# A decoder step's feed-forward: sums moved between engines, a product block that starts on a copied bank, and a new ordering rule

## The chip, the cores and the metric

The kernel runs on one core of one Trainium2 chip. The metric is the device time of one execution in microseconds (us), as the median of several runs. The engines go by the names of the profile: PE multiplies matrices, ACT, DVE and POOL are the scalar, vector and general-purpose engines, SP starts most transfers. PSUM is the memory that PE writes its products to, in eight banks; SBUF is the working memory.

## What is computed

One step of a decoder layer for 512 prompt tokens and 32 sample tokens together (544 columns; the width is 1024). First come a mixing layer (attention and a recurrence) and a cross attention, which this change does not edit. Then follows the feed-forward, cut here from the reference:

```
u    = rmsnorm(x, norm_ffn)
ug   = u @ w_gate                              # 1024 x 2816
up   = concatenate([conv_buf, ug])
conv = conv_b + sum(conv_w[j] * up[:, j:j + T] for j in range(3))
x    = x + (silu(conv) * (u @ w_up)) @ w_down  # w_up 1024 x 2816, w_down 2816 x 1024
y    = rmsnorm(x, norm_final)
```

## The kernel before

Activations lie transposed, features on partitions and tokens along the free axis. Every fp32 product is made as three products in the faster fp32r format: each operand is split into a high part (a cast, on ACT) and a low part (operand minus high part, on DVE), and PE adds up high x high, high x low and low x high.

The 2816 hidden features are 22 tiles of 128. The first four gate tiles and the first four up tiles (`PLAIN`) are made directly: two halves of 256 and 288 columns each, 24 matmuls a half, with the row factor `r_ffn` (tile `r_ux` in the profile) put in when the bank is read. The other 18 gate and 18 up tiles are made in pairs (class `Pair`), by a seven-product scheme for 2x2 blocks: instead of eight block products, q1 to q7, 12 matmuls each, of which some use sums of blocks. On the activation side the blocks are called B11, B12, B21, B22, and the sums X, T, U, V (`blocks`, L1899); each is 128x544 in each of two parts `kp`. They are made once. Six tensors in each part need a high and a low part, and so does T. In the kernel before, the sums T and V and the low parts of T, V and B22 run on POOL (`ON_GPSIMD`, L1898), the rest on DVE. On the weight side S1 and S3 are added up by a transfer that accumulates, which POOL starts, and S2 and S4 by DVE.

Of a pair's outputs c11 = q1 + q2: ACT copies q1 out of bank `a` into SBUF (`kept`), q2 goes to a bank of its own (`d`), and DVE adds the two into the output tile. The block c12 is copied by ACT out of bank `a` (`c12_out`). c22 and c21 are made by DVE out of bank `c` and a kept copy. Bank `a` runs on: q1, q6, q5 and q3 all add up in it, with copies taken between. These banks come from a kind of five (`aux`); the down products use three others.

A gate tile then passes `conv` (L1760): a first tap on ACT, two taps on DVE, silu on ACT (tile `cv` in the profile). For the last tile the silu is recorded as one step with a load of the activation table set `LN_SET`, which the closing norm uses (L1778). An up tile passes `gated` (L1786): the product with the gate on POOL, 512 columns and 32 columns apart, then the split into h high and low. Last come the products with `w_down`, in groups of hidden tiles (`DOWNS`), as halves of 256 and 288 columns that DVE adds to x (tile `xr`), and for tiles 18 to 21 a closing stage (`last_half`, banks `ps_dz`) with the closing norm (`final`): a sum of squares over partitions on PE, Ln and Exp on ACT (`r_fin`, `r_final`), the products with y on DVE and POOL, and the transfers out.

**What sets the order.** The kernel is not emitted as written. Class `Tape` records every call as a step, with its tiles, an estimate of its length and its dependences. PE's main products keep the order in which they were recorded; for the feed-forward that order, `seq`, is written out by hand at the end (L2070 on). Everything else is ordered by a simulation in the recorder (`order`, L439): each engine starts the step that is due first (`begin`), due times run backwards from the products (`due`), and a step may start once it is due within its `lead` (15 us, or a value given for loads and splits). The simulation runs three times, each with the product times of the one before, and the last order is emitted. It also holds a picture of the SBUF port that DVE and POOL share: a DVE step of two kinds (`tensor_scalar`, `scalar_tensor_tensor`, with no PSUM operand) waits until POOL is free.

All of this happens before the launch; on the chip each engine runs its list in order and waits on semaphores. A tile that the change touches can therefore move others.

Of the kernel before, what the change touches and what calls it, by code (L numbers as in the profile page):

```python
# [17 lines left out]
SEQ = 512  # L18
# [231 lines left out]
class Tape:  # L250
# [7 lines left out]
    ROUNDS = 3  # L258
    BURST, PATIENCE, SLACK, LEAD = 1.0, 4.0, 12.0, 15.0
# [123 lines left out]
    def due(self):  # L383
# [18 lines left out]
        for s in reversed(self.steps):  # L402
            for u in s.users:
                if s in u.deps and not s.main:
                    s.begin = min(s.begin, u.begin - s.takes())

    def run(self):
# [3 lines left out]
        for s in self.mains:  # L411
            s.est = t
            t += s.length * scale
        for _ in range(self.ROUNDS):
            done = self.order()
            for s in self.mains:
                s.est = s.start
        for s in done:
            for call in s.calls:
                call()  # L420
# [3 lines left out]
    def order(self):  # L424
# [21 lines left out]
        now, clock, bus, todo, done, burst, first = 0.0, [0.0, 0.0], 0.0, len(self.steps), [], False, None  # L446

# [28 lines left out]
        def start(s):  # L476
# [13 lines left out]
            else:  # L490
                held_up = max(0.0, free["POOL"] - now) if s.port else 0.0
# [27 lines left out]
        while todo:  # L519
# [4 lines left out]
            for e in ("SP", "ACT", "DVE", "POOL"):  # L524
                if free[e] <= now + 1e-9:
                    at = clock[0] + min(now - clock[1], 4.0)
                    can = [s for s in waiting[e] if s.ready <= now + 1e-9 and s.begin <= at + (s.lead or self.LEAD) and fits(s)]
                    if can:
                        busy = free["POOL"] > now + 0.1
# [38 lines left out]
class _Engine:  # L568
# [5 lines left out]
    def __getattr__(self, method):  # L574
# [3 lines left out]
        def take(*args, **kw):  # L578
# [38 lines left out]
def tile_decoder_step(ctx: ExitStack, tc: tile.TileContext, xT, memT, kwT, vw, s0, conv_in, mkT, mv, vecs, cst,  # L617
# [1089 lines left out]
    dense_by_half(co_hl, KT, "co", co_evac, co_after)  # L1707
# [52 lines left out]
    def conv(j, deps):  # L1760
# [24 lines left out]
    def gated(j, deps):  # L1785

        def product():
            up, c = ups[j], hid[j]
            nc.gpsimd.tensor_tensor(up[:, :SEQ], up[:, :SEQ], c[:, :SEQ], op=ALU.mult)

        def product_s():
            up, c = ups[j], hid[j]
            nc.gpsimd.tensor_tensor(by_batch(up[:, SEQ:N]), by_batch(up[:, SEQ:N]), seg(c)[:, :, 0:4], op=ALU.mult)
# [8 lines left out]
        hi = job(high, job(product, *deps), job(product_s, *deps))  # L1802
# [3 lines left out]
    def load_a(name, src, k, lead=4.0):  # L1806
# [8 lines left out]
    def load_sum(name, a, b):  # L1815

        load, box = load_a(name, a, 4, lead=3.0)
# [3 lines left out]
        return job(lambda: None, job(accumulate, load, lead=4.0)), box  # L1821

    def split_a(name, box, k, ready, lead=6.0):
# [27 lines left out]
    def plain_tile(kind, j, i):  # L1851
# [3 lines left out]
        else:  # L1855
            load = job(lambda: ws.load(i, True), lead=9.0)
            split = job(lambda: ws.split_lo(i), job(lambda: ws.split_hi(i), load, lead=5.0),
                        lead=5.0)
        start = job(new_tile(kind, j), lead=6.0)
# [38 lines left out]
    ON_GPSIMD = ('T', 'V', 'B22')  # L1898

    def blocks(kp):  # L1900
# [27 lines left out]
        def low(name):  # L1928
            (nc.gpsimd if name in ON_GPSIMD else nc.vector).tensor_tensor(split(name, "l"), tok[name, kp]["t"], tok[name, kp]["h"].bitcast(F32),
# [14 lines left out]
    class Pair:  # L1944


        def __init__(self, kind, j, gates):
# [22 lines left out]
            first = job(load, lead=5.0)  # L1970
# [6 lines left out]
            for out, a, b in (("S2", "S1", "A11"), ("S4", "S2", "A12")):  # L1977
                self.w[out] = {}
                made[out] = job(lambda o=(out, a, b): self.add(*o), made[a], made[b], lead=8.0)
            self.low["A11"] = self.low["A12"] = job(low, job(high, first, lead=8.0), lead=8.0)  # L1980
# [243 lines left out]
```

## Time and profile before

| what | us |
|---|---|
| median of 3 runs | 848.43 (847.07 to 849.92) |
| the profiled execution | 845.8 |
| its span | 843.6 |
| PE busy in the span | 819.0 |
| DVE, ACT, POOL busy | 593.9, 403.6, 207.2 |
| activation table loads, 16 | 20.5 in all |

The profiled execution has 2.2 us around its span. A page of the profile gives the busy time of each engine, then the chain of work that ended last; further views group instructions by shape, list who waited for whom, or list the instructions in order of time. In a row of such a list the first number is the start, the second the duration, and what stands in brackets is how long the engine stood idle before it and whose end released it. Almost all instructions have the line of one helper (L612), so rows are told apart by the names of their tiles. As a guide to time: the mixing layer and the cross attention run to about 450 us, the plain tiles and the block sums to about 515, the pairs with the down products to about 806, and the closing stage to the end.

### The profile page before, as it was taken

To read this page: it belongs to the slowest core of one execution; us is meant where nothing else is said; L and a number is where in the kernel's file an instruction comes from. 1 tells how busy PE (TensorE), PEld (TensorE's weight loads), DVE (VectorE), ACT (ScalarE), POOL (GpSimd) and SP (SyncE) were. 2 spreads that over 40 slices of the span, in tenths; PEclk is the share of its full clock that TensorE was granted. 3 is DMA by queue.
4 is the path that set the end of the run, shared out by engine and by line. 5 is a ranking of instruction groups with operands and counts; after the bars stand their busy time and mean duration, and the time that the engine had idled before them with its cause. 6 is when DMAs were issued, how large, how long until landed. Compare 5 with 4: busy or idle time off the path is not lost.

```text
span 843.6 us, 18802 instructions
## 1 busy us (share of the span) xinstructions
PE 819.0 (97%) x7594; PEld 766.1 (91%) x7594; DVE 593.9 (70%) x1201; ACT 403.6 (48%) x798; POOL 207.2 (25%) x293
## 2 busy tenths in 40 slices
PE   9999999999999989999999988999999999999894
PEld 9989977888789879999889988999999999999894
DVE  6783735875988896564667987877867867768843
ACT  7412333543456454444545545454544634646625
POOL 1220000210210220222224863213222332333213
PEclk9999999999999999999999999999999999999998
DMA  9656797957932625260721345445565565465203
GB/s 333 210 137 191 251 293 244 302 158 226 302 87 77 206 79 187 61 220 23 247 85 50 95 132 137 131 123 150 149 150 139 138 162 148 128 175 162 74 1 107
DMA packets 90759, 132.32 MB, mean 157 GB/s; under 512 B 6064, under 2 KB 60080, under 8 KB 90544
## 3 DMA queue, kind: packets, MB, share of 16 engines
q1 hardware_dynamic: 84480, 120.69, 44.6%
q0 software_dynamic: 5184, 9.44, 6.9%
q8 instruction: 59, 0.97, 0.4%
q10 hardware_dynamic: 1008, 0.99, 0.3%
q14 instruction: 28, 0.23, 0.1%
HBM read 123.03 MB, written 8.07 MB: 155 GB/s over the span
## 4 chain that ended last, share of the span: by engine, by line
PE 81%; DVE 11%; ACT 3%; issue 2%; DMA 2%; POOL 1%; SPq 0%; DVEq 0%; POOLq 0%; ACTq 0%
PE ps_d L612 12%; PE ps_ag L612 6%; PE ps_wo L612 6%; PE ps_au L612 6%; PE ps_hv L612 3%; PE ps_k L612 3%; PE ps_co L612 3%; PE ps_cq L612 3%; PE ps_cu L612 3%; PE ps_cg L612 3%; PE ps_v L612 3%; PE ps_hq L612 2%; PE ps_hg L612 2%; PE ps_dz L612 2%; PE ps_hf L612 2%
## 5 line engine op out<-in xcount | busy, mean ns | idle before, releaser
L612 ACT CAST wh<-wr 128x1024 fp32r<-128x1024 f32 (+1 forms) x68 | 60.9, 908 | 102.0 <-PE ps_k L612 16.9
L612 POOL TENSOR_TENSOR up<-up,cv 128x512 f32<-128x512 f32 (+1 forms) x44 | 45.8, 1051 | 138.9 <-ACT cv L612 109.6
L612 DVE TENSOR_TENSOR wl<-wr,wh 128x1024 fp32r<-128x1024 f32 (+1 forms) x68 | 71.9, 1068 | 10.4 <-ACT wh L612 10.3
L612 POOL TENSOR_TENSOR hG<-hG,hf 128x256 f32<-128x256 f32 (+1 forms) x28 | 26.1, 933 | 189.8 <-DVE hf L612 134.9
L612 DVE TENSOR_TENSOR xr<-xr,ps_d 128x256 f32<-128x256 f32 x80 | 34.4, 433 | 25.4 <-PE ps_d L612 24.7
L612 DVE SCALAR_TENSOR_TENSOR cv<-ug,vec,cv 128x560 f32<-128x560 f32 x44 | 37.5, 853 | 1.5 <-ACT cv L612 1.1
L612 POOL COPY last<-ug 128x16 f32<-128x16 f32 (+1 forms) x44 | 15.6, 402 | 72.2 <-ACT ug L612 57.5
L612 ACT ACTIVATE cv<-cv 128x560 f32<-128x560 f32 x22 | 14.8, 674 | 30.5 <-DVE cv L612 30.5
L612 POOL TENSOR_TENSOR acc_cx<-acc_cx,sq_cx 128x256 f32<-128x256 f32 (+1 forms) x14 | 11.7, 839 | 56.5 <-ACT sq_cx L612 56.4
L612 ACT ACT_TABLE_LOAD x16 | 20.5, 1283 | 2.4 <-issue 2.2
L612 ACT ACTIVATE cv<-ug,vec 128x560 f32<-128x560 f32 x22 | 18.9, 860 | 3.9 <-POOL ug L612 2.8
L612 ACT ACTIVATE P<-P,mx 128x128 f32<-128x128 f32 (+3 forms) x32 | 17.6, 551 | 4.5 <-DVE mx L612 4.4
L612 PE MATMUL ps_co<-coh,wh 128*128 128x256 f32 (+1 forms) x64 | 18.9, 295 | 0.0
L612 PE MATMUL ps_co<-coh,wl 128*128 128x256 f32 (+1 forms) x64 | 18.4, 288 | 0.0
L612 PE MATMUL ps_co<-col,wh 128*128 128x256 f32 (+1 forms) x64 | 18.4, 288 | 0.0
L612 DVE TENSOR_TENSOR xr<-xr,ps_wo 128x256 f32<-128x256 f32 (+1 forms) x16 | 6.8, 435 | 15.1 <-PE ps_wo L612 15.1
L612 POOL COPY ug<-conv_state 128x16 f32<-128x16 f32 x22 | 17.1, 782 | 0.0
L612 ACT COPY keptu<-ps_au 128x272 f32<-128x272 f32 x18 | 7.0, 389 | 20.3 <-PE ps_au L612 19.6
L612 POOL TENSOR_TENSOR acc_ux<-acc_ux,sq_ux 128x256 f32<-128x256 f32 (+1 forms) x14 | 11.5, 820 | 20.4 <-ACT sq_ux L612 20.4
L612 PE MATMUL psd<-st,qbd_win 128*32 128x224 f32 x256 | 15.6, 359 | 0.0
L612 DVE TENSOR_TENSOR kq<-hq,hf 128x256 f32<-128x256 f32 (+1 forms) x28 | 15.3, 548 | 0.0
L612 PE MATMUL psdo<-st,dpt 128*32 128x256 f32 x224 | 15.3, 385 | 0.0
(2650 smaller groups left out, 3577.5 us busy)
## 6 DMA issues: line engine op xcount, KB each, us to landing
st<-in_kwT SPq DMA_DIRECT2D x32, 448.0 KB, 5.4
st<-in_vw SPq DMA_DIRECT2D x28, 512.0 KB, 5.6
wr<-in_w_in SPq DMA_DIRECT2D x25, 512.0 KB, 5.5
wd<-in_w_down SPq DMA_DIRECT2D x32, 256.0 KB, 4.1
wrg<-in_w_gate SPq DMA_DIRECT2D x9, 512.0 KB, 3.8
wru<-in_w_up SPq DMA_DIRECT2D x9, 512.0 KB, 5.8
st<-in_mkT SPq DMA_DIRECT2D x8, 512.0 KB, 6.1
wr<-in_w_out SPq DMA_DIRECT2D x8, 512.0 KB, 4.1
```

Of the source, the lines that this page charges most:

```text
L612: return tape.put(engine, lambda: call(*args, **kw), outs, ins, length, lag, size, port)
```

## The change

- **Block sums.** T, V and the low parts of T, V and B22 go to DVE, so all block sums and their low parts are on DVE.
- **First products.** ACT copies q1 into PSUM, a bank `d`, and q2 adds up onto that copy (no `start`). c11 is then read straight from bank `d` (`direct`). A burst of five matmuls (`mark_banks`), recorded second in the order of the feed-forward, writes each of the five aux banks once beforehand.
- **Gate from PSUM.** For the even up tile of a pair, c11 and c12 are multiplied with the gate as DVE reads them from PSUM, so no product in SBUF follows. For a gate tile c11 and c12 are ACT copies. The odd tiles keep their path, but their product, like that of the plain tiles, runs on DVE.
- **Order of products.** In a pair's turn q2 and the q3 of the pair before change places; the first pair's q1 moves ahead of the last plain half.
- **Table set.** The load of `LN_SET` is taken out of the last silu's step and recorded in the closing stage, gated on its last product of the first half.
- **Row factor.** The sum for the first half of the feed-forward's norm becomes a main product, right after the second half of output block 1 of the cross attention, instead of an extra product.
- **Recorder.** Four rounds, of which the one with the earliest simulated end of PE is emitted. A step that feeds a main product directly is due 4 us earlier (`MARGIN`). Leads of loads and splits in the feed-forward grow by 8 us; the closing stage's weight loads and splits get a lead of 12. The port picture covers every DVE step without a PSUM operand, and holds DVE behind POOL and POOL behind DVE.

```diff
-    ROUNDS = 3
-    BURST, PATIENCE, SLACK, LEAD = 1.0, 4.0, 12.0, 15.0
+    ROUNDS = 4
+    BURST, PATIENCE, SLACK, LEAD, MARGIN = 1.0, 4.0, 12.0, 15.0, 4.0
...
-                    s.begin = min(s.begin, u.begin - s.takes())
+                    s.begin = min(s.begin, u.begin - s.takes() - self.MARGIN * u.main)
...
         for _ in range(self.ROUNDS):
             done = self.order()
+            end = max(s.end for s in done if s.engine == "PE")
+            if best is None or end < best[0]:
+                best = end, done
...
-                held_up = max(0.0, free["POOL"] - now) if s.port else 0.0
+                held_up = max(0.0, port[s.engine == "DVE"] - now) if s.port else 0.0
+                if s.port:
+                    port[s.engine == "POOL"] = now + held_up + s.length
...
-                port = method in ("tensor_scalar", "scalar_tensor_tensor") and not any(
-                    tape.kinds.get(a.tensor.name) in ("dense", "aux", "dec") for a in aps)
+                port = not any(tape.kinds.get(a.tensor.name) in ("dense", "aux", "dec") for a in aps)
             else:
+                port = True
...
         ffn_in.take(m, int(n0 > 0))
-
-    def co_after(m, c):
-        if m == KT - 1 and c == 0:
-            ffn_in.rows(0)
+        if m == 1 and n0:
+            with tape.main():
+                ffn_in.rows(0)
...
-            with tape.together():
-                nc.scalar.activation(hid[j][:, :W], hid[j][:, :W], AF.Silu)
-                if j == FT - 1:
-                    nc.scalar.preload_act_table_set(LN_SET)
+            nc.scalar.activation(hid[j][:, :W], hid[j][:, :W], AF.Silu)
...
-            nc.gpsimd.tensor_tensor(up[:, :SEQ], up[:, :SEQ], c[:, :SEQ], op=ALU.mult)
+            nc.vector.tensor_tensor(up[:, :SEQ], up[:, :SEQ], c[:, :SEQ], op=ALU.mult)
...
-    ON_GPSIMD = ('T', 'V', 'B22')
...
-            on = nc.gpsimd if name in ON_GPSIMD else nc.vector
-            on.tensor_tensor(place(name), tok[a, kp]["t"], tok[b, kp]["t"], op=op)
+            nc.vector.tensor_tensor(place(name), tok[a, kp]["t"], tok[b, kp]["t"], op=op)
...
             q1 = self.product("a", "A11", "B11", True)
             q = self.keep("q", q1)
-            q2 = self.product("d", "A12", "B21", True)
-            c11 = self.out(kind, j, 0, "q", "d", ALU.add, q, q2, start[0])
+            q2 = self.product("d", "A12", "B21", False, q)
+            c11 = self.direct(kind, j, 0, "d", q2, start[0], *gates[0:1])
...
-            c12 = job(c12_out, q3, start[0])
+            c12 = self.direct(kind, j, HT, "a", q3, start[0], *gates[0:1])
...
-            self.done = [do(j, [c11, c12] + gates[0:1]), do(j + 1, [c21, c22] + gates[1:2])]
+            self.done = [do(j, [c11, c12], False), do(j + 1, [c21, c22] + gates[1:2], True)]
...
                 if name == "q":
+                    out = self.s["d"] = PX(f"ps_d{self.name}")
...
+        def direct(self, kind, j, n0, bank, *deps):
+
+            def fn():
+                for out, of in places(kind, j, n0, HT):
+                    if kind == "g":
+                        nc.scalar.copy(out, of(self.s[bank]))
+                    elif n0 == 0:
+                        nc.vector.tensor_tensor(out, of(self.s[bank]), hid[j][:, :HT], op=ALU.mult)
+                    else:
+                        m = SEQ - HT
+                        nc.vector.tensor_tensor(out[:, :m], self.s[bank][:, :m], hid[j][:, HT:SEQ], op=ALU.mult)
+                        nc.vector.tensor_tensor(by_batch(out[:, m:HT]), by_batch(self.s[bank][:, m:HT]),
+                                                seg(hid[j])[:, :, 0:4], op=ALU.mult)
+            return job(fn, *deps)
...
     seq = later.order[:4 * PLAIN]
+    seq.insert(-1, units[0].q.pop(1))
+
+    def mark_banks():
+        for i in range(5):
+            nc.tensor.matmul(PX(f"ps_mark{i}")[:, :HT], ux[0][0][:, :128], ux[0][0][:, :HT], start=True, stop=True)
+
+    later.pe(mark_banks)
+    seq.insert(1, later.order.pop())
...
-        for part, room in zip(((1, 2), (3, 6), (7, 4), (5,)), per):
+        for part, room in zip(((1, 3), (2, 6), (7, 4), (5,)), per):
...
             nc.sync.dma_start(conv_out, last2)
+            nc.scalar.preload_act_table_set(LN_SET)
...
-        nc.sync.dma_start(t, w_down[m][:, 128 * DOWN_LAST[0]:128 * DOWN_LAST[1]].rearrange("p (k c) -> p k c", c=128))
-        nc.scalar.copy(hi, t)
-        nc.vector.tensor_tensor(lo, t, hi.bitcast(F32), op=ALU.subtract)
+        with tape.early(12.0):
+            nc.sync.dma_start(t, w_down[m][:, 128 * DOWN_LAST[0]:128 * DOWN_LAST[1]]
+                              .rearrange("p (k c) -> p k c", c=128))
+            nc.scalar.copy(hi, t)
+            nc.vector.tensor_tensor(lo, t, hi.bitcast(F32), op=ALU.subtract)
```

More of the change, by code (lines that the diff above doesn't have):

```diff
@@ L413, in run @@
             t += s.length * scale
+        best = None
         for _ in range(self.ROUNDS):
             done = self.order()
+            end = max(s.end for s in done if s.engine == "PE")
+            if best is None or end < best[0]:
+                best = end, done
             for s in self.mains:
                 s.est = s.start
-        for s in done:
+        for s in best[1]:
             for call in s.calls:
@@ L446, in order @@
         now, clock, bus, todo, done, burst, first = 0.0, [0.0, 0.0], 0.0, len(self.steps), [], False, None
+        port = [0.0, 0.0]
         def needs(s):
@@ L528, in order @@
                     if can:
-                        busy = free["POOL"] > now + 0.1
+                        busy = port[e == "DVE"] > now + 0.1
                         start(min(can, key=lambda s: (s.begin + 2.0 * (s.port and busy), s.number)))
@@ L1758, in places, with conv @@
         return found
-    def conv(j, deps):
+    def conv(j, deps, _=True):
         def first():
@@ L1855, in plain_tile @@
         else:
[L1856 to L1859, printed above, removed]
+            load = job(lambda: ws.load(i, True), lead=17.0)
+            split = job(lambda: ws.split_lo(i), job(lambda: ws.split_hi(i), load, lead=13.0),
+                        lead=13.0)
+        start = job(new_tile(kind, j), lead=14.0)
         done = []
@@ L1968, in low @@
                     self.w[n]["l"] = lo[:, k:k + 4, :]
-            first = job(load, lead=5.0)
+            first = job(load, lead=13.0)
             loads = {"A11": first, "A12": first}
@@ L1978, in __init__ @@
                 self.w[out] = {}
-                made[out] = job(lambda o=(out, a, b): self.add(*o), made[a], made[b], lead=8.0)
-            self.low["A11"] = self.low["A12"] = job(low, job(high, first, lead=8.0), lead=8.0)
+                made[out] = job(lambda o=(out, a, b): self.add(*o), made[a], made[b], lead=16.0)
+            self.low["A11"] = self.low["A12"] = job(low, job(high, first, lead=16.0), lead=16.0)
             for n in ("S2", "S3", "S1", "S4", "A22"):
                 self.low[n] = split_a(n + self.name, self.w[n], 4, made[n])
-            start = [job(new_tile(kind, j + i), lead=6.0) for i in range(2)]
+            start = [job(new_tile(kind, j + i), lead=14.0) for i in range(2)]
             q1 = self.product("a", "A11", "B11", True)
             q = self.keep("q", q1)
-            q2 = self.product("d", "A12", "B21", True)
-            c11 = self.out(kind, j, 0, "q", "d", ALU.add, q, q2, start[0])
+            q2 = self.product("d", "A12", "B21", False, q)
+            c11 = self.direct(kind, j, 0, "d", q2, start[0], *gates[0:1])
             q6 = self.product("a", "S2", "U", False, q)
@@ L1995, in __init__ @@
             q3 = self.product("a", "S4", "B22", False, r)
-            def c12_out():
-                for out, of in places(kind, j, HT, HT):
-                    nc.scalar.copy(out, of(self.s["a"]))
-            c12 = job(c12_out, q3, start[0])
+            c12 = self.direct(kind, j, HT, "a", q3, start[0], *gates[0:1])
             q4 = self.product("c", "A22", "V", False, c22)
@@ L2026, in fn @@
                 if name == "q":
+                    out = self.s["d"] = PX(f"ps_d{self.name}")
+                elif name == "z":
                     self.s["kept"] = A(f"kept{self.name}")
[L2028 to L2032 removed]
+                    out = self.s["z"] = self.s["kept"][:, :HT]
+                else:
+                    out = self.s["r"] = self.s["kept"][:, HT:2 * HT]
+                nc.scalar.copy(out[:, :HT], self.s["a"][:, :HT])
             return job(fn, q)
+        def direct(self, kind, j, n0, bank, *deps):
[11 more added lines that the diff above has]
+            return job(fn, *deps)
         def out(self, kind, j, n0, a, b, op, *deps):
```

22 lines of the change are left out of this document (9 added, 13 removed).

## The prediction

> **What bounds the kernel now.** I read the page first, then the busy time by stage, then what PE waited for.
>
> ```profile
> span 843.6 us, 18802 instructions
> ...
> PE 819.0 (97%) x7594; PEld 766.1 (91%) x7594; DVE 593.9 (70%) x1201; ACT 403.6 (48%) x798; POOL 207.2 (25%) x293
> ...
> 0.00:450.00 450.00, 443.91 (x4630) 393.70 (x4631) 301.32 (x713) 203.79 (x436) 73.12 (x99) 1.00 0.57 184
> 450.00:515.00 65.00, 59.43 (x466) 58.37 (x465) 58.56 (x82) 32.73 (x50) 40.45 (x39) 1.00 0.39 106
> 515.00:795.00 280.00, 280.00 (x2235) 280.00 (x2234) 213.27 (x361) 144.98 (x276) 78.48 (x136) 1.00 0.55 144
> 795.00:806.00 11.00, 8.88 (x71) 8.67 (x70) 8.25 (x18) 5.40 (x7) 3.80 (x4) 1.00 0.01 1
> 806.00:844.00 38.00, 26.76 (x201) 25.33 (x199) 12.55 (x30) 16.66 (x31) 11.37 (x15) 0.92 0.18 60
> ...
> PE ps_ag L612 <- ACT keptg L612: 3.1, 2, 2.0
> PE ps_g L612 <- DVE wl L612: 2.2, 1, 2.2
> PE ps_d L612 <- DVE xr L612: 2.1, 1, 2.1
> ```
>
> A stage's row gives its length, then the busy time of PE, of its weight loads, of DVE, ACT and POOL. PE is busy 819.0 of 843.6 us, and its granted clock (the third number from the end) is full up to the closing stage. From 515 to 795 it has no gap. The change takes no product away and adds five matmuls, so it can win only where PE stands idle: 65 - 59.43 = 5.57 us in the stage of the block sums, 11 - 8.88 = 2.12 just before the closing stage, and in the closing stage, which ends in a chain without PE. The 6.1 us before 450 lie in stages whose code is hardly edited. Of the waits the first two are in the stage of the block sums; the third is the whole of the 2.12.
>
> **Block sums (450 to 515).** DVE is busy 58.56 of 65 us, but part of that is time in which POOL holds it:
>
> ```profile
> L612 DVE SCALAR_TENSOR_TENSOR B<-xr,vec,r_ux 128x272 f32<-128x272 f32 x16 | 10.1, 682 | 1.2 <-ACT r_ux L612 1.2
> L612 DVE SCALAR_TENSOR_TENSOR cv<-ug,vec,cv 128x560 f32<-128x560 f32 x8 | 8.9, 1110 | 1.2 <-ACT cv L612 1.1
> ...
> L612 DVE TENSOR_TENSOR Ul<-U,Uh 128x544 fp32r<-128x544 f32 x2 | 3.3, 1647 | 0.0
> L612 DVE TENSOR_TENSOR U<-X,B 128x544 f32<-128x544 f32 x2 | 3.0, 1500 | 0.0
> L612 DVE TENSOR_TENSOR B21l<-B,B21h 128x544 fp32r<-128x544 f32 x2 | 2.5, 1256 | 0.0
> ...
> L612 DVE TENSOR_TENSOR X<-B,B 128x544 f32<-128x544 f32 x2 | 1.4, 712 | 0.0
> ...
> L612 DVE SCALAR_TENSOR_TENSOR B<-xr,vec,r_ux x16: 490/496/1612, 455.1 to 484.2; 128x272 f32<-128x272 f32 x16
> ...
> L612 DVE SCALAR_TENSOR_TENSOR cv<-ug,vec,cv x44: 785/796/1782, 469.7 to 795.5; 128x560 f32<-128x560 f32 x44
> ```
>
> Undisturbed, 128x544 takes 0.712 us (X), the medians of B and cv are 0.496 and 0.796. The excess is 16 x (0.682 - 0.496) = 3.0 for B, 8 x (1.110 - 0.796) = 2.5 for cv, 2 x (1.647 - 0.712) = 1.9 for Ul, 1.6 for U, 1.1 for B21l: 10.1 us. Onto DVE move ten block operations (T, V, Tl, Vl, B22l, twice each), 7.1 us at 0.712, and four plain products with the gate, which DVE doesn't show; at X's rate for 512 columns (0.67) and a piece of 32 columns, 0.8 each, 3.2. Together 10.3 us more against up to 10.1 less. How strict the hold is:
>
> ```profile
> 464.03 2.19 POOL L612 TENSOR_TENSOR T<-B,B 128x544 f32<-128x544 f32 x1 [1.21 <-DVE B L612]
> ...
> 465.29 1.51 DVE L612 TENSOR_TENSOR U<-X,B 128x544 f32<-128x544 f32 x1
> ```
>
> T ends at 466.22, and U, which needs 0.71, at 466.80: it made hardly any progress before T was done. So the excess is a matter of POOL's work being there, and I let 9 of the 10.1 go with it; POOL keeps small copies. The Trainium skill (SBUF — State Buffer, Who interferes with whom) states this as a rule: two-input DVE work contends with POOL's reads, and whoever issues first has the shared port pair for the whole instruction; by it the whole 10.1 would go and the sum be 1.1 us lower, and the rows of T and U agree. DVE's load stays about as it was. What is won is order and latency, as in the longest wait:
>
> ```profile
> 498.10 2.49 POOL L612 TENSOR_TENSOR up<-up,cv 128x512 f32<-128x512 f32 x2 [4.93 <-ACT cv L612]
> 500.53 0.88 POOL L588 DMA_DIRECT2D S3g<-in_w_gate  x1
> ...
> 505.31 0.62 ACT L612 CAST S3g4h<-S3g 128x512 fp32r<-128x512 f32 x1 [1.02 <-DMA S3g<-in_w_gate]
> ...
> 506.78 0.38 ACT L612 COPY keptg<-ps_ag 128x272 f32<-128x272 f32 x1
> ```
>
> POOL waited 4.93 us for a silu, with the accumulating transfer of S3 queued behind it. The transfer came late, ACT's cast waited for it, and behind the cast stood the copy of q1 that PE wanted. In the new kernel POOL has no such product ahead of the transfer, loads are due earlier (SP's queue keeps its order, so a load still waits if one ahead waits for a buffer), and q1 lies a plain half, some 3 us, ahead of q2. So the 3.1 us behind keptg should go, and of the 2.2 behind `wl`, where DVE stays full, a small part. I take **-3.5 us**. Ends: -5.6 with every gap closed; +5.3 if only half the excess goes and DVE has no slack (10.3 - 5.0).
>
> The five marking matmuls stand behind the first plain half:
>
> ```profile
> 513.32 1.51 PE ps_au L612 x12
> ...
> 453.25 0.75 PE L612 MATMUL psr_ux<-acc_ux,cs 128*128 128x288 f32 x2
> ...
> 454.04 0.50 ACT L612 ACTIVATE r_ux<-psr_ux,eps 128x288 f32<-128x288 f32 x1 [2.00 <-PE psr_ux L612]
> ...
> 438.85 0.74 POOL L612 TENSOR_TENSOR acc_ux<-acc_ux,sq_ux 128x256 f32<-128x256 f32 x1 [0.69 <-ACT sq_ux L612]
> ```
>
> At 1.51/12 each they take 0.63. They need all five aux banks at once, and the norm's sum (453.25) sits in one until ACT has read it at 454.54: up to 1.3 more. Ends 0.6 and 1.9; as part of it falls into gaps that DVE leaves anyway, **+1.0**. The first half's sum of squares, now a main product, finds its last addition done at 439.6, before the second half of output block 1 is through; it costs nothing, and half a microsecond if the squares came later.
>
> **Pairs (515 to 795).** PE is full, so nothing is won. In each round of a gate and an up pair DVE loses the addition for c11 and gains c12 in two pieces and one product of 0.8: about 0.9 us more (an estimate: c12's read is as long as the addition that goes, the small piece is 0.1 and the product 0.8) in a round of some 33 us (280 us hold eight and a half rounds), on a load of 213.27/280, 76%, with POOL's products out of its way. ACT gains one copy. ACT writing its copy to PSUM is not in this stage; the nearest row is keptg's 0.38, and q2 has q3 and a down half, some 3 us, between itself and q1. I cost the stage at **0**; what could break it is the first rival.
>
> **Before the closing stage.**
>
> ```profile
> 795.92 2.57 ACT L612 ACT_TABLE_LOAD   x2
> ...
> 799.50 1.30 DVE L612 TENSOR_TENSOR wd_7l<-wd,wd_7h 128x256 fp32r<-128x256 f32 x1 [1.88 <-ACT wd_7h L612]
> ```
>
> `LN_SET` is loaded with the silu of tile 21, and tile 20's silu comes after it: two loads, 2.57 us, for nothing. ACT's cast of wd_7 stood behind them, DVE's subtraction waited 1.88 us for it, the additions to x queued behind that, and PE ran out of down banks: the 2.12 us. Without the loads none of this is late; the gate of tile 20 is also done earlier, and the closing weights' splits no longer crowd DVE there. **-2.1** (ends -2.1 and 0, if DVE's extra product takes the place).
>
> **Closing stage.**
>
> ```profile
> 825.85 1.28 ACT L612 ACT_TABLE_LOAD   x1
> ...
> 834.10 1.28 ACT L612 ACT_TABLE_LOAD   x1
> 835.39 0.47 ACT L612 ACTIVATE r_fin<-psr_final,eps 128x256 f32<-128x256 f32 x1
> 835.88 1.28 ACT L612 ACT_TABLE_LOAD   x1
> ...
> 827.60 0.94 DVE L612 SCALAR_TENSOR_TENSOR y<-xr,vec,r_final 128x288 f32<-128x288 f32 x2 [4.09 <-ACT r_final L612]
> ...
> 828.92 0.39 PE L612 MATMUL ps_dz<-h18h,wdhz 128*128 128x256 f32 x1 [0.66 <-DVE xr L612]
> ...
> 831.74 0.28 PE L612 MATMUL ps_dz<-h21h,wdlz 128*128 128x256 f32 x1
> ...
> 833.22 0.41 DVE L612 TENSOR_TENSOR xr<-xr,ps_dz 128x256 f32<-128x256 f32 x1
> ```
>
> Because of the wasted load the set is gone when the norm comes: Ln loads one, Exp another, in both halves. With `LN_SET` loaded once, about when the last product of the first half starts, while ACT is mostly idle (16.66 of 38 us busy in the stage), all four vanish. The last two lie on the last path: 2 x 1.28 = 2.56. The first two kept DVE waiting 4.09 us for r_final with the additions to x behind it, so PE stalled 0.66 and the last addition came at 833.22, though PE's last product ended at 832.02: without that some 0.66 + 1.1. **-4.3** (ends -4.5 and -2.6). Row and rule differ on a load's price: here Ln starts at 835.39, 0.01 after its load. The Trainium skill (ScalarE: Activation LUTs, What ACT_TABLE_LOAD costs) adds a drain of about 1.38 us to every switch; no row here shows a gap for it.
>
> **Sum:** -3.5 + 1.0 - 2.1 - 4.3 = -8.9 on a span of 843.6, so 834.7, and 836.9 with the 2.2 us around the span. The profiled execution (845.8) lies 2.6 under the median 848.43, so the median should come to **839.5**. About 2.5 us (0.3%) can be told from no change.
>
> **Rivals.**
> - *The gate held in PSUM stalls the pairs.* From q3 a silu needs a PSUM copy (0.38), the rows below, and two taps at 0.80:
>
> ```profile
> L612 ACT ACTIVATE cv<-ug,vec x22: 853/857/872, 466.9 to 791.2; 128x560 f32<-128x560 f32 x22
> L612 ACT ACTIVATE cv<-cv x22: 671/673/679, 473.1 to 798.5; 128x560 f32<-128x560 f32 x22
> ```
>
>  That is 3.5 us and four hand-offs, while q2 ends 3 us after q3. DVE then waits perhaps 1 us at c11, which three down banks cover. Were each of nine up pairs to cost PE one product time (1.51), that is 13.6 us: 853. It decides above 1 us a pair (8.9/9). Against it: DVE has a quarter of its time free, and the recorder makes PSUM reads due at once. Chance 0.09.
> - *DVE stays the bound in the block sums.* Half the excess stays, some of it finds slack: +1 instead of -3.5, so 844. For it: DVE is busy 58.56 of 65 us; against it, T and U. 0.17.
> - *The table load lands badly* (in front of the norm's Ln, or sets are loaded again): the -4.3 is lost, 844. Against it: the first norms run Ln and Exp without loads after such a preload. 0.05.
> - *A switch costs more than its load's row*, a stop of ACT that the load's row doesn't hold. By the rows it is 0.01 us behind the load, so by them the time stays at 839.5; 0.04 that they hide something, on the faster side. By the Trainium skill's drain (the section named above) the last path would lose 2 x 1.38 us more, and the time would be 836.7.
> - *The new order shifts the stages before 450*, where DVE works 301 of 450 us and order decides 6.1 us of waits: losing as much again and more cancels the gain, 848. The new port rule is nearer to the rows, so I give it 0.07.
>
> **Numbers.** Forecast 0.58, 839.5, its own range 835 to 844. The range 834.5 to 847 takes in the rivals but the first and half of the last. Faster: 0.58, of the second rival 0.12, the third 0.05, the fourth 0.04, the last 0.01: 0.80. Within 0.3%: 0.03 + 0.01 + 0.05 = 0.09. Slower: 0.08 + 0.02 + 0.01 = 0.11.
>
> **What would show it.** Right: after the last silu one table load only, between the two halves of the closing stage; PE idle under 3 us from 450 to 515 and near none from there to the closing stage; U and Ul near 0.71; Ln and Exp back to back. Wrong: PE waiting for bank `d` or a down bank among the pairs, DVE full and U still at 1.5, or PE idle much above 6.1 us before 450.

## The result and the profile after

The new kernel takes **840.7 us** (median of 6 runs, 837.55 to 842.07) against 847.22 us of the kernel before in runs made together (6 runs, 845.83 to 849.92): a ratio of 0.9916, 95% interval 0.9891 to 0.9941, or 6.5 us less. The forecast was 839.5 us. The total fits, but the stages do not all fit. Here is the new kernel's page, and its busy time in the same stages as before (length, then PE, weight loads, DVE, ACT, POOL; the third number from the end is PE's granted clock):

```profile
span 837.3 us, 18858 instructions
...
PE 820.8 (98%) x7599; PEld 768.2 (92%) x7599; DVE 584.8 (70%) x1246; ACT 398.9 (48%) x793; POOL 139.0 (17%) x239
```

```profile
0.00:450.00 450.00, 442.39 (x4606) 392.14 (x4607) 299.68 (x710) 202.16 (x433) 69.25 (x96) 1.00 0.57 185
450.00:515.00 65.00, 64.65 (x513) 64.34 (x512) 53.50 (x99) 34.24 (x55) 13.80 (x28) 1.00 0.40 113
515.00:795.00 280.00, 278.61 (x2218) 277.96 (x2218) 210.59 (x392) 147.00 (x275) 44.52 (x100) 1.00 0.55 142
795.00:806.00 11.00, 11.00 (x88) 10.86 (x87) 9.18 (x21) 2.84 (x6) 0.00 (x0) 1.00 0.01 2
```

PE's idle time from 450 to 806 was 5.57 + 2.12 = 7.7 us and is 0.35 + 1.39 = 1.7 us. Ahead of 450 it grew, from 6.1 to 7.6 us. The list of what PE waited for shows with what:

```profile
PE psA L621 <- issue: 5.2, 3, 2.2
PE ps_first L621 <- DVE zero L621: 1.1, 1, 1.1
PE ps_au L621 <- ACT S2u4h L621: 0.8, 1, 0.8
PE psdo L621 <- DMA st<-in_vw: 0.7, 1, 0.7
PE ps_hf L621 <- issue: 0.5, 1, 0.5
```

The waits for `keptg`, for `wl` and for the down bank are gone. At the top stands one that names no engine: "issue", three times, at the small products `psA` of the mixing layer (32 columns), code that the change does not edit.

It is clearest to cut each span at two products of PE: the first plain product (`ps_g`) and the first product of the closing stage (`ps_dz`). The profiles of the kernels below, but for two whose start was changed, in us:

| kernel | up to `ps_g` | `ps_g` to `ps_dz` | `ps_dz` to the end | span | time against before |
|---|---|---|---|---|---|
| before | 450.4 | 355.5 | 37.7 | 843.6 | |
| after | 453.6 | 349.9 | 33.8 | 837.3 | 0.9916 |
| after, again | 452.6 | 350.0 | 33.8 | 836.5 | 0.9906 |
| a_front | 450.1 | 348.4 | 33.8 | 832.3 | 0.9828 |
| b_recorder | 454.7 | 358.7 | 34.6 | 848.0 | 1.0010 |
| b_table | 449.5 | 355.6 | 34.5 | 839.6 | 0.9929 |
| b_sums | 451.2 | 355.1 | 37.7 | 844.0 | 0.9970 |
| b_prod | 450.7 | 351.6 | 34.7 | 837.0 | 0.9886 |
| b_dve | 449.9 | 349.5 | 33.9 | 833.3 | 0.9866 |
| a_pool | 448.4 | 360.8 | 33.8 | 843.1 | 0.9967 |
| a_noseed | 448.0 | 348.1 | 33.9 | 830.0 | 0.9832 |
| a_oldtab | 447.7 | 348.7 | 33.9 | 830.2 | 0.9831 |

So after against before: +3.2, -5.6, -3.9. The closing stage of after shows the step that was costed closest, one load of 1.28 us, placed while ACT has time, and Ln and Exp with no load between:

```profile
814.18 1.28 ACT L621 ACT_TABLE_LOAD   x1
...
821.61 0.50 ACT L621 ACTIVATE r_fin<-psr_final,eps 128x288 f32<-128x288 f32 x1
822.14 0.41 ACT L621 ACTIVATE r_final<-r_fin 128x288 f32<-128x288 f32 x1
...
830.41 0.47 ACT L621 ACTIVATE r_fin<-psr_final,eps 128x256 f32<-128x256 f32 x1 [0.79 <-PE psr_final L621]
830.91 0.39 ACT L621 ACTIVATE r_final<-r_fin 128x256 f32<-128x256 f32 x1
```

And DVE's block sums run undisturbed (mean of one in ns after the comma; U was 1500, Ul 1647, B 682, cv 1110):

```profile
L621 DVE SCALAR_TENSOR_TENSOR B<-xr,vec,r_ux 128x272 f32<-128x272 f32 x16 | 7.3, 495 | 0.0
L621 DVE SCALAR_TENSOR_TENSOR cv<-ug,vec,cv 128x560 f32<-128x560 f32 x8 | 6.4, 795 | 0.1
L621 DVE TENSOR_TENSOR U<-X,B 128x544 f32<-128x544 f32 x2 | 1.4, 716 | 0.0
...
L621 DVE TENSOR_TENSOR Ul<-U,Uh 128x544 fp32r<-128x544 f32 x2 | 1.4, 718 | 0.0
```

### The profile page after: what moved, and what is told of

It reads as the page before. It is cut to its first block, busy times and chain, and to the rows that moved or that the text cites. A ratio compares the mean times of both kernels' runs of the same rounds, so it can differ in the third digit from the quotient of the medians.

```text
span 837.3 us, 18858 instructions
## 1 busy us (share of the span) xinstructions
PE 820.8 (98%) x7599; PEld 768.2 (92%) x7599; DVE 584.8 (70%) x1246; ACT 398.9 (48%) x793; POOL 139.0 (17%) x239
## 4 chain that ended last, share of the span: by engine, by line
PE 94%; DMA 3%; ACT 1%; issue 1%; DVE 0%; ACTq 0%; DVEq 0%
PE ps_d L621 13%; PE ps_au L621 6%; PE ps_ag L621 6%; PE ps_wo L621 6%; PE ps_cu L621 3%; PE ps_cg L621 3%; PE ps_k L621 3%; PE ps_q L621 3%; PE ps_hv L621 3%; PE ps_co L621 3%; PE ps_cq L621 3%; PE ps_g L621 3%; PE ps_dz L621 3%; PE ps_v L621 3%; PE ps_u L621 3%; PE ps_hf L621 2%
## 5 line engine op out<-in xcount | busy, mean ns | idle before, releaser
L621 DVE SCALAR_TENSOR_TENSOR cv<-ug,vec,cv 128x560 f32<-128x560 f32 x44 | 35.1, 797 | 8.1 <-ACT cv L621 7.8
L621 POOL COPY last<-ug 128x2 f32<-128x2 f32 (+1 forms) x44 | 13.6, 340 | 160.7 <-DVE ug L621 133.5
L597 POOL DMA_DIRECT2D S1u<-in_w_up x9 | 7.8, 862 | 87.6 <-DMA S1u<-in_w_up 31.0
L621 DVE TENSOR_TENSOR xr<-xr,ps_dz 128x288 f32<-128x288 f32 (+1 forms) x16 | 7.0, 436 | 12.4 <-PE ps_dz L621 12.4
L621 POOL TENSOR_TENSOR acc_ux<-acc_ux,sq_ux 128x256 f32<-128x256 f32 (+1 forms) x14 | 11.9, 848 | 20.8 <-ACT sq_ux L621 20.8
L621 DVE CUSTOM_DVE_ANT_0 P<-psS,bias 128x128 f32<-128x128 f32 (+3 forms) x32 | 14.2, 484 | 1.4 <-PE psS L621 1.3
## 6 DMA issues: line engine op xcount, KB each, us to landing
st<-in_kwT SPq DMA_DIRECT2D x32, 448.0 KB, 5.0
```

Source lines behind the costliest of these rows:

```text
L597: return tape.put(engine, lambda: call(*args, **kw), outs, ins, 0.1, 0.3, size)
L621: return tape.put(engine, lambda: call(*args, **kw), outs, ins, length, lag, size, port)
```

## Experiments

The theory that went into them: the stages from 450 on gained what the prediction says, for its reasons; what was lost ahead of 450 comes from the recorder's new port picture, which puts the steps there in another order. The rivals: the loss is chance; the gains belong to other edits than the prediction named.

### Is the loss ahead of 450 real, and whose is it?

**after_again** is the new kernel unchanged.

> The changed kernel unchanged, for the spread. Theory (the new order costs the stages before the feed-forward 3.3 us): the first plain product starts at 453.7 us again, within 0.7, the span is 837 within 1, and PE waits some 5 us for nothing visible at the small products psA. Rival (the 3.3 us were this execution's luck): the start lies anywhere from 450 to 454 and the waits at psA are another sum.

839.74 us (6 runs), ratio 0.9906 (0.9885 to 0.9927); `psA` waits on issue for 5.1 us, three times, longest 2.4. It is not chance.

**a_front**: the new rules hold only for steps recorded from the cross attention's output on.

```
+    tape.cut()
+    tape.fresh = True
     def co_evac(m, ps, n0, n):
...
+                if s.fresh:
                     held_up = max(0.0, port[s.engine == "DVE"] - now) if s.port else 0.0
+                else:
+                    held_up = max(0.0, free["POOL"] - now) if s.port else 0.0
```

> The changed kernel with the recorder's old port picture and no margin for all steps recorded before the output projection of the cross attention; the feed-forward keeps the new rules. Theory: the stages before the feed-forward are as in the kernel before, the first plain product starts at 450.4 within 1 us, and the span is 834, 3.3 us under the changed kernel. Rival (luck): no difference beyond 1 us.

832.22 us (832.05 to 835.45, 5 runs), ratio 0.9828 (0.9805 to 0.9851): 7.5 us less than the new kernel in the same runs, and **the fastest version found** (the expectations below call it the improved version; two variants of it, a_noseed and a_oldtab, can't be told apart from it). `ps_g` starts at 450.1, and PE has one issue wait, of 2.2 us. In the profiles the gain is 5.0 us, 3.5 up to `ps_g` and 1.5 behind it. The profiled execution (834.09 us, span 832.3, mean granted clock 0.996) has a stretch at half clock right behind that wait; the three fastest runs have spans of 830.3 to 830.5 at a mean clock of 0.997 or 0.998, so they seem to have been spared it. With the margin left in for those early steps too (a kernel that was not run), PE's, ACT's and POOL's lists of instructions come out the same and two rows of DVE's differ: the order ahead of 450 is the port picture's doing.

**b_recorder**: the kernel before with the recorder's rules alone.

> The kernel before with the recorder's rules alone (four rounds and the best of them, the margin, the port both ways); no edit of the feed-forward. Theory: the stages before the feed-forward get 3.3 us longer with waits at psA of about 5 us, the feed-forward gains at most 2, so 1 to 3 us slower than before. Rival (luck): 450.4 within 1 us for the first plain product and no difference in time.

849.0 us (12 runs), ratio 1.0010 (0.9994 to 1.0026). The rules by themselves cost 4.3 us up to `ps_g` (issue waits at `psA` 5.5 us, three times) and 3.2 us in the middle, where PE waits 3.4 and 2.5 us for S2 and S3 splits, and they give back 3.1 us in the closing stage, because the new order happens to put the table load behind both of the last silus. The rules are no gain for the old kernel.

### What are the issue waits?

A list of the instruction transfers in the trace (59 packets of 16,384 bytes on a queue of their own) shows that these gaps of PE follow such a packet. Columns: start of the product after the gap, the gap, the tile, its number among PE's matmuls, and how long before it an instruction packet landed (all us):

```
before     230.03  1.71  psA   #2638  1.34
after       49.14  1.92  psA   #478   1.28
after      171.36  1.07  psA   #1877  1.42
after      177.04  0.49  ps_hf #2004  1.41
after      235.83  2.21  psA   #2640  1.31
a_phase     73.66  1.51  psA   #606   1.22
a_phase    195.83  1.05  psA   #2005  1.57
a_phase    201.53  0.51  ps_hf #2132  1.52
a_phase    261.07  2.99  psA   #2768  1.22
a_half     178.66  0.55  ps_v  #1877  1.28
a_half     184.93  2.43  psL   #2004  1.45
a_half     308.41  2.00  psA   #3402  1.36
```

**a_phase** adds 64 matmuls to the warm-up at the start, so that packets end at other products.

```
+            tape.put("PE", lambda: [tc.nc.tensor.matmul(bank, zero[:, :128], zero[:, :16], start=True, stop=True)
+                                    for _ in range(64)], [bank], [zero[:, :128]], 0.0)
```

> The kernel after, with 64 more matmuls of 16 columns among the warm-up matmuls at its start and nothing else: all other lists of instructions stay the same. 59 packets of PE's instructions carry 0.97 MB for some 15,200 matmuls and weight loads, so 64 bytes each; 64 matmuls with their weight loads are 8,192 bytes, half a packet of 16,384. Theory (the issue waits at the small products psA come where a packet of instructions is fetched late, just then): the packets now end at other products, so the 5.1 us at psA shrink to under 3 or move to other tiles. Rival (they come from the new order, bursts of small matmuls wherever the packets end): three waits at psA again, 4.5 to 5.5 us. The extra matmuls themselves may put the start off by up to some 4 us, so the total says little: 838 to 844.

The waits were the same three at `psA`, 5.5 us, and the whole is some 24 us longer (863.67 us), nearly all of it at the added products, which ran at a granted clock of 0.50 from 9.36 us on:

```profile
5.49 24.23 PE L935 MATMUL ps_first<-zero 128*128 128x16 f32 x128
```

By the expectation the three waits spoke for the rival, but the experiment had a flaw: the trace shows 128 more matmuls, not 64, since each ran in two passes. 128 matmuls and 128 loads are exactly one packet, so nothing moved, and indeed each stall lies 128 matmuls later in the list above (478 to 606, 1877 to 2005, 2004 to 2132, 2640 to 2768). **a_half** puts this right with 32.

> As the run with 64 more warm-up matmuls, but 32 of them. That run was no test: each of the 64 was carried out in two passes, 128 matmuls and 128 weight loads, 256 instructions of 64 bytes, exactly one packet of 16,384, so the packets ended where they had ended. 32 give 8,192 bytes, half a packet. Theory (the issue waits come where a packet ends inside or near a burst of small matmuls): the waits at psA change, in sum by more than 1 us from 5.2 to 5.5, or move to other tiles. Rival (any burst of these small products outruns the fetching, wherever a packet ends): three waits at psA, 4.5 to 5.8 us, at the same products. The start is some 12 us later, so the total says nothing: 848 to 853.

851.6 us, one run, some 12 us of it again at the start.

```profile
PE psL L621 <- issue: 2.4, 1, 2.4
PE psA L621 <- issue: 2.0, 1, 2.0
PE psd L621 <- DMA st<-in_kwT: 1.5, 1, 1.5
...
PE ps_v L621 <- issue: 0.6, 1, 0.6
```

The stalls moved to other tiles, and two of them stand at matmuls #1877 and #2004 of the stream as in after, though other products have these numbers now. They are tied to packet ends: #1877 and #2004 are 127 apart, one packet. The sum of the issue waits (5.0, against 5.7 with `ps_hf`) hardly changed. The number alone does not decide. In before, #1877 falls among `psA` products too, and PE runs on: the packet there landed at 162.98 us and PE came to the product at 166.45. In after it landed at 169.94, PE was through with what it had at 170.28, and the next product started at 171.36. So a packet that comes late costs, and in the listed gaps the first product starts 1.2 to 1.6 us after it has landed. Why packets come late in the new order is argued, not shown: products of 32 columns use up instructions fastest (before ran 62 of `psA` in 0.72 us), and ahead of #478 two tiles of them, `psB` and `psA`, now follow each other, where the old order had `psd` and `ps_q` between. What sets the time at which a packet is asked for, no run shows. The Trainium skill (Runtime: NRT & Kernel Launch, Instruction fetch mechanics) has the instructions refilled in blocks of 16 KiB, 256 instructions, with a cost that is mostly hidden. The size agrees with these packets; among small products it is not hidden here, 0.5 to 3.0 us a time.

The gap brings a second loss. Around the longest `psA` wait of after:

```profile
235.83 0.38 PE L621 MATMUL psA<-kq 128*32 128x32 f32 x10 [2.21 <-issue]
```

```profile
230.00:234.00 4.00, 3.62 (x173) 2.77 (x172) 3.27 (x8) 2.17 (x4) 0.67 (x1) 1.00 1.10 362
234.00:236.00 2.00, 0.17 (x11) 0.17 (x14) 1.45 (x5) 0.00 (x0) 0.70 (x1) 0.85 1.15 333
236.00:238.00 2.00, 2.00 (x21) 1.62 (x18) 0.49 (x2) 0.25 (x1) 0.63 (x1) 0.50 0.79 279
238.00:240.00 2.00, 2.00 (x15) 2.00 (x15) 0.00 (x0) 0.00 (x0) 0.00 (x0) 0.79 0.03 12
```

The granted clock falls to 0.50 from 235.4 to 238.8. PE runs again from 235.83, so it loses half of 3.0 us, 1.5. The kernel before has its 1.71 us wait at this place, and the clock stays 1.00. So the 3.2 us ahead of 450 are 1.5 of idle time (6.1 to 7.6) and 1.5 of clock, and 0.2 is left over.

### Who gained what behind 450?

**b_dve**: the kernel before with all block sums and gate products on DVE. **b_sums** and **b_prod** are its two halves. PE's and SP's lists are those of before in all three.

```
-    ON_GPSIMD = ('T', 'V', 'B22')                       # b_dve, b_sums
+    ON_GPSIMD = ()
...
-            nc.gpsimd.tensor_tensor(up[:, :SEQ], ...)   # b_dve, b_prod
+            nc.vector.tensor_tensor(up[:, :SEQ], ...)
```

> The kernel before with one part of the change: all block sums, their low parts and the products with the gate run on VectorE; leads, ordering rules and PE's order are the old ones. Theory (the excess on VectorE was POOL holding the shared port, and the transfer of S3 stood behind a POOL product): U and Ul near 0.72 us, the 3.1 us wait at ps_ag behind keptg shrinks, and the time falls by 2 to 3.5 us, to 844 to 845.5. Rival (the gain of that stage comes from longer leads and from q1 moved ahead): U at 0.72 too, but the waits for keptg and wl stay above 4 us together, and the time within 1 us of before.

835.16 us (5 runs), ratio 0.9866 (0.9844 to 0.9888): 11.9 us less than before, nearly twice what the whole change brings, and far outside both expectations.

> The kernel before with the block sums and their low parts alone on VectorE; the products with the gate stay on GpSimd, PE's and SP's orders are unchanged, and the recorded order still has two loads of the activation table before the last silu. Theory (both kinds of POOL work hold the shared port, and the product waits ahead of the transfer of S3): U and Ul at 0.72, the wait for keptg stays near 3 us, the closing stage stays near 37.5 us, and the time falls by 1 to 3 us: 844 to 846. Rival (the sums carry nearly all of the 11.9 us that both moves together gave): 837 to 840.

845.05 us (12 runs), ratio 0.9970 (0.9959 to 0.9982): -2.5 us. All 16 table loads are still there, PE still waits 2.8 us for `keptg` and 2.2 us at a down bank, and U still takes 1.275 us on average.

> The kernel before with the products with the gate alone on VectorE; the block sums stay on GpSimd, PE's and SP's orders are unchanged. In the recorded order tile 20's silu now comes ahead of tile 21's, so the table is loaded once, behind both. Theory: U and Ul stay near 1.5, the closing stage shrinks from 37.5 to about 34 us as with the table load moved by itself, the 2.1 us ahead of it go, and keptg is shorter: 837 to 841. Rival (the products carry nothing, the sums do): 844 to 847.

838.01 us (4 runs), ratio 0.9886 (0.9869 to 0.9903): -9.6 us. Middle -3.9 and closing stage -3.0 in the profile. The busy time from 450 on, first b_sums, then b_prod, then b_dve:

```profile
450.00:515.00 65.00, 62.22 (x482) 61.80 (x481) 57.53 (x95) 33.59 (x52) 24.30 (x32) 0.97 0.41 112
...
795.00:806.00 11.00, 8.85 (x59) 8.64 (x58) 7.08 (x16) 4.54 (x6) 3.69 (x4) 0.84 0.01 1
```

```profile
450.00:515.00 65.00, 60.91 (x477) 59.87 (x476) 60.64 (x93) 35.09 (x54) 31.27 (x34) 1.00 0.43 114
...
795.00:806.00 11.00, 11.00 (x88) 11.00 (x87) 8.19 (x22) 4.00 (x6) 0.00 (x0) 1.00 0.01 2
```

```profile
450.00:515.00 65.00, 62.81 (x498) 62.18 (x497) 58.29 (x107) 34.69 (x54) 16.79 (x23) 1.00 0.43 114
515.00:795.00 280.00, 280.00 (x2234) 280.00 (x2233) 216.40 (x397) 144.88 (x275) 50.25 (x102) 1.00 0.55 142
795.00:806.00 11.00, 11.00 (x88) 11.00 (x87) 5.95 (x17) 2.96 (x6) 1.39 (x2) 1.00 0.00 0
```

b_dve leaves 65 - 62.81 = 2.2 us of idle in the block sums, where before had 5.57, and none ahead of the closing stage. The measured halves add up, 2.5 + 9.6 against 11.9, and the products carry four fifths.

The rows tell more than the totals. In the block sums the sums bring the larger part: PE's idle time falls from 5.57 to 65 - 62.22 = 2.78 us with them and to 65 - 60.91 = 4.09 with the products, and POOL issues the first transfer of S3 2.7 us earlier after `ps_g` in b_sums, 0.8 in b_prod. But b_sums keeps two waits:

```profile
PE ps_ag L612 <- ACT keptg L612: 2.8, 1, 2.8
PE ps_d L612 <- DVE xr L612: 2.2, 1, 2.2
```

Behind each of them the clock is 0.50 for 3.41 us, hence the 0.97 and the 0.84 in its rows. That loses some 1.7 us each time, so that the profile of b_sums is no shorter than that of before (844.0 and 843.6 us). Over all their runs both kernels have a median granted clock of 0.993, and there the 2.5 us measured lie near the 2.8 us of idle time that went. The products' larger part lies at the end. Without them on POOL the recorder finishes tile 20's silu ahead of tile 21's, and the table load, although still in the last silu's step, comes behind both. In b_prod:

```profile
792.97 0.67 ACT L612 ACTIVATE cv<-cv 128x560 f32<-128x560 f32 x1
...
795.10 0.68 ACT L612 ACTIVATE cv<-cv 128x560 f32<-128x560 f32 x1 [1.16 <-DVE cv L612]
795.79 1.28 ACT L612 ACT_TABLE_LOAD   x1
```

**b_table**: the kernel before with the table load alone moved.

```
-                if j == FT - 1:
-                    nc.scalar.preload_act_table_set(LN_SET)
...
             nc.sync.dma_start(conv_out, last2)
+            nc.scalar.preload_act_table_set(LN_SET)
```

> The kernel before with the load of the table set moved into the closing stage, nothing else; PE's order is that of before. By the prediction's terms: the 2.1 us wait before the closing stage goes and the closing stage is 4.3 us shorter (3.8 as the changed kernel shows it), so 5.9 to 6.4 us in all, 841. Rival (the 2.1 us come from DVE's crowding, not from the loads): 3.8 us only, and PE still waits some 2 us for DVE before the closing stage.

841.65 us (6 runs), ratio 0.9929 (0.9908 to 0.9949): -5.8 us.

```profile
450.00:515.00 65.00, 58.73 (x461) 57.68 (x460) 59.14 (x82) 32.15 (x49) 38.41 (x40) 1.00 0.41 106
...
795.00:806.00 11.00, 9.97 (x76) 9.43 (x76) 9.53 (x19) 2.51 (x6) 3.55 (x4) 1.00 0.00 1
```

In the profile the closing stage is 3.2 us shorter and the middle unchanged: ahead of the closing stage PE's idle time falls from 2.12 to 1.03 us (`h21h` and `xr` still late), and in the block sums it is 65 - 58.73 = 6.3 us, 0.7 more than before.

**a_oldtab**: a_front with the table load put back into the last silu's step.

> The improved version with the table load back in the last silu's step, as before the change. With the products on VectorE the recorded order already has tile 20's silu ahead of it. Theory (the two edits bring the same gain, which counts once): one load, four loads of the closing stage gone all the same, 831.5 to 833.5. Rival (the edit of the table load is needed for itself): the closing stage near 37 us, 835 to 838.

833.14 us (4 runs), ratio 0.9831 (0.9814 to 0.9849), the same as a_front: one load, right behind the last silu.

```profile
785.07 0.67 ACT L627 ACTIVATE cv<-cv 128x560 f32<-128x560 f32 x1 [0.59 <-DVE cv L627]
785.77 1.28 ACT L627 ACT_TABLE_LOAD   x1
```

So in a_front the edit of the table load brings nothing that its other edits had not brought; by b_prod the moved products alone are enough for that, and by b_recorder the recorder's rules alone.

**a_pool**: a_front with T, V and the low parts of T, V and B22 back on POOL. PE's order is a_front's; for that the order of the recorder's second round is emitted.

> The improved version (old port picture and no margin ahead of the feed-forward) with the block sums T and V and the low parts of T, V and B22 back on GpSimd, PE's order unchanged. Theory (POOL's work is the excess): U and Ul back near 1.5 us, B near 0.68, and PE idle from 450 to 515 rises from 0.05 us to 2 to 3.5: 834 to 836. Rival (early loads and the moved q1 make that stage, POOL's work is hidden): the long rows come back as well, but PE idle there stays under 1 us: 832 to 833.

844.82 us (11 runs), ratio 0.9967 (0.9953 to 0.9981): 12.6 us more than a_front (11.8 by the two ratios, since the runs were not made together), where the theory had 2 to 3.5, and U and Ul stay at 0.72, against the theory. Most of the cost sits in one DVE instruction. DVE, POOL and PE around it:

```profile
505.04 7.78 DVE L627 TENSOR_TENSOR wlu<-wru,whu 128x1024 fp32r<-128x1024 f32 x1
```

```profile
505.13 2.95 POOL L627 TENSOR_TENSOR B22l<-B,B22h 128x544 fp32r<-128x544 f32 x2
...
508.36 1.92 POOL L627 TENSOR_TENSOR V<-B,U 128x544 f32<-128x544 f32 x1
...
509.82 1.91 POOL L627 TENSOR_TENSOR Vl<-V,Vh 128x544 fp32r<-128x544 f32 x1
```

```profile
512.88 0.59 PE L627 MATMUL ps_au<-B11h,wlu 128*128 128x272 f32 x1 [5.92 <-DVE wlu L627]
```

```profile
512.00:522.00 10.00, 8.13 (x33) 7.59 (x34) 6.61 (x12) 4.84 (x10) 4.93 (x9) 0.50 0.33 109
```

The same instruction took 1.21 us in a_front. Here it ends 1.09 us after the last POOL sum (511.73), so by the rows four POOL sums went ahead of it one after another. PE stood 5.92 us and then ran at half clock to 522, which costs some 4 us more: together most of the 12.4 us by which the middle is longer than in a_front.

**a_noseed**: a_front without the copied bank, the gate from PSUM and the marks.

```
-            q2 = self.product("d", "A12", "B21", False, q)
-            c11 = self.direct(kind, j, 0, "d", q2, start[0], *gates[0:1])
+            q2 = self.product("d", "A12", "B21", True)
+            c11 = self.out(kind, j, 0, "q", "d", ALU.add, q, q2, start[0])
...
-    later.pe(mark_banks)
-    seq.insert(1, later.order.pop())
```

> The improved version without the copied bank: q2 starts a bank of its own, VectorE adds q1 and q2, ScalarE copies c12, the product with the gate runs on VectorE from SBUF, and the five marking matmuls are left out; the order of the products is unchanged. Theory (the copied bank and the reads from PSUM cost and save nothing, since PE is full in the pairs either way; the marks cost their 0.63 us): PE idle among the pairs under 0.5 us and the time 831.3 to 832.3. Rival (they take needed load off VectorE): PE idle among the pairs rises by 2 us or more, 834 to 837.

833.47 us (5 runs), ratio 0.9832 (0.9812 to 0.9851), the same as a_front. PE is full in the pairs:

```profile
515.00:795.00 280.00, 280.00 (x2234) 279.86 (x2233) 215.55 (x403) 143.78 (x269) 40.87 (x94) 1.00 0.53 137
```

The middle is 348.1 against 348.4 us. The span is 2.3 us shorter, but that is the front: `psA` waits 1.4 us there and the clock holds, in a_front 2.2 us and it does not. PE's list up to `ps_g` is the same in both.

## Why the prediction was right, and where not

- **Total.** -8.9 was forecast on the span; it was -6.3 (843.6 to 837.3). That the time came within 1.2 us of the forecast all the same is in part luck: the median lies 3.4 us above the profiled span, where the forecast added 4.8 as in before. The step that failed is "stages before 450 at nothing": it cost 3.2 us. The fifth rival named the place, but only as an event that cancels the whole gain, and it took the new port rule as a reason to give it no more than 0.07; by a_front and b_recorder that rule is what cost the time. A term of its own, worked out from the small products there and PE's issue wait of 1.7 us in the trace of before, was due.
- **Block sums, -3.5, marks +1.0, gap -2.1: together -4.6; measured -5.6.** U and Ul came to 0.72 as foretold, and PE's idle time in the block sums fell to 0.35 us, so the term came out near its end of -5.6 rather than at -3.5. The reasons hold in part. The excess of the sums (T holding U), on which the prediction put the weight, is the larger half in that stage: 2.8 us of idle time go in b_sums, and its time falls by 2.5. The move of the products, whose place ahead of S3 was the example for the waits, takes 1.5 us of idle time there in b_prod; most of what it brings lies behind this stage.
- **Marks.** Five in 0.63 us were forecast. They take that time on PE, and the middle of a_noseed, which has none, is 0.3 us shorter than a_front's: smaller than +1.0.
- **Pairs at 0.** Right: a_noseed and a_front do not differ, and no wait for bank `d` or for a PSUM gate appears. The first rival, 853 us, did not come. PE lost 1.39 us from 515 to 795, waiting for S2u's splits and h3's at the very start.
- **Ahead of the closing stage, -2.1.** The size is right, the cause half right: without the two loads alone (b_table) 1.03 of the 2.12 us stay. The products on DVE remove all of it (b_prod).
- **Closing stage, -4.3; measured -3.9.** The mechanism is right, two loads out of the last chain and DVE not kept waiting; the term was 0.4 us too large. That the edit of the table load brings it is shown by b_table for the old kernel (3.2 us) and refuted for the new rules by a_oldtab: the other edits give the same order without it.
- **DVE stays the bound** did not happen: 53.50 of 65 us busy, PE idle for 0.35. The price that POOL's sums can have is seen in a_pool.
- **A switch costs more than its load's row.** b_table, with all four loads of the closing stage gone, saves 3.2 us there, less than the 4.3 that the rows gave. No run asks for a further 1.38 us a switch.

One term is missing from the account so far. The profiled execution of before lies 2 us under its median, so that the profile differences of b_prod (-6.6) and b_table (-4.0) are smaller than the measured ones (-9.6 and -5.8). The granted clock of the other runs on record tells most of why. In the 50 runs of before that were made beside the experiments its mean is 0.989 to 0.996, with a median of 0.993; in the profiled execution it is 0.997. One stretch of 3.41 us at half clock lowers the mean by 0.002, so a typical run has about two such stretches that the profile has not, at up to 1.7 us each. The spans agree: 843.9 us on average in the nine runs at 0.995 or 0.996, 847.5 in the seven at 0.989 to 0.991. All four runs of b_prod have 0.997. Part of its gain is thus that waits of some 2 us, which at times cost the clock, are gone.

What stays open: which of the three waits of 2.0 to 2.2 us in before pays for the clock, and how often, no profile of before shows. And a_front is still some 3 us under b_dve (ratios 0.9828 and 0.9866); whether the new order of products, the longer leads, the row factor or the rules inside the feed-forward bring that was not run.

## What to carry to other kernels

Test an ordering rule by itself before it goes in with other edits: here it cost more than the copied bank, the marks and the table edit brought on top of the moved products, and confining it to the feed-forward gave 7.5 us. When two edits aim at one stage, ask whether the first already gives what the second is for; a gain that hangs on the order of two instructions can be had by whatever changes that order. Cost also the stages that are not edited if the order of their work can move, and look there for PE waits that name no engine. Compare the granted clock of many runs as well as one profile: the profiled execution of before was spared a cost that most of its runs paid.

## What the runs showed of the hardware

- **PE's clock after a gap.** It drops to 0.50 in windows of 3.41 us, or of 10.24 us, three times as long. In the profiles of before, after and the experiments every gap of PE of 2.21 us or more between its products came with one, which began in the gap or up to 1.7 us behind it (ten: the shortest in after, 2.25 in a_front, 2.78 in b_sums, 2.99 in a_phase; 10.24 us long behind the 3.36 of b_recorder, which takes in its next gap of 2.55, and behind the 5.92 of a_pool). Of seven gaps from 2.00 to 2.16 us two did (2.00 in a_half, 2.15 in b_sums), three of before and one each of b_table and b_sums did not; shorter ones with work right behind them did not. A wait that grows from 2.0 to 2.3 us can thus cost some 1.5 us more than itself. A gap is not the only way: in a_phase the clock was 0.50 from 9.36 to 33.26 us, seven times 3.41, while PE's rows show no gap; up to 29.72 us they are products of 16 columns. The Trainium skill (TensorE: Matmul & The Clock Gate, Part 1) gives the window as 3.41 us, which agrees, and lets the clock fall after at least one idle window; here a gap of 2.2 us, less than one window, was enough.
- **One DVE instruction can be held by several POOL instructions in a row** (7.78 us for 1.21 in a_pool), though its row starts 0.09 us ahead of the first of them. By these rows the hold is not one POOL instruction long (one case, and spans on POOL are rough). The same sums cost some 2 to 3 us in the old order (2.5 between before and b_sums, 1.7 by the ratios of b_prod and b_dve) and some 12 in the new one; that this depends on how closely POOL's list is packed is argued from the rows of a_pool, not tested.
